# A transformer block on one core: the second feed-forward product with tokens on partitions, and the last norm along the row

## The chip, the cores and the metric

The kernel runs on one NeuronCore of a Trainium2 chip. The metric is the device time of one execution in microseconds, as the median of three runs. PE is the tensor engine (PEld its weight loads), DVE the vector engine, ACT the scalar engine, POOL GpSimd, and SP the engine whose queue issues the loads.

## The reference

One block on 256 tokens of 1024 features, all in float32. What matters here is its end:

```python
    h = rmsnorm(x, g_ffn[l]) * (1 + scale2) + shift2
    x = x + gate2 * (jnp.square(jax.nn.relu(h @ w_ff1[l])) @ w_ff2[l])   # 1024 -> 4096 -> 1024
return rmsnorm(x, g_final)                                              # per token, times g_final per feature
```

`gate2` is a vector over the 1024 features (a product of a condition vector with a weight matrix). Ahead of it stand a first norm, attention in one block of 256 keys, a gated unit and an output projection.

## The kernel before

Activations lie turned: features on partitions, tokens in the row. `x_sb` is 128 x (8, 256): eight feature tiles of 256 tokens. Every weight chunk of 128 x 2048 float32 (1 MB) is loaded by SP into `raw` (five buffers), rounded by ACT to `whi`, and the rest is taken by DVE as `wlo`; activations are split in the same way, and `mm3` adds three products in the rounded type: high by high, high by low, low by high.

The feed-forward runs in 16 units of 256 hidden features. `ff1` makes one unit's hidden sums (48 products of 258 columns), `relu2` turns them on DVE and ACT into `fh`, `relu2_low` into `fl`, each 128 x (2, 256), and `ff2` adds that unit's part of the second product to four banks `acc` that stay open over all units. The order on PE is written out in the loop: `ff1` of unit n + 3 follows `ff2` of unit n. Of one unit, `ff2` before makes 48 products: for each of eight feature tiles and two halves of the hidden features, 128 x 128 of the weight is the stationary operand, and 256 tokens of `fh` or `fl` are streamed.

```python
            for i in range(2):
                w = slice(1024 * i + P * ft, 1024 * i + P * ft + P)
                mm3(o, wh[:, w], wl[:, w], fh[:, i], fl[:, i], first and i == 0 and ft % 2 == 0,
                    last and i == 1, skip_group_check=ft % 2 == 1)
```

The last two units run by pairs of feature tiles, so that one bank after the other is complete. After each bank DVE adds gate times sum to `x_sb`, ACT squares it, and the final gain is applied per partition (`yg`). Then sixteen transposes on PE put tokens on partitions, products of one column by `ones` add the squares over the features, `rstd` takes 1/rms on ACT and POOL, and ACT and DVE each scale two quarters of the output (`ys`), which SP stores in four DMAs.

Engines issue their instructions in order. In the first part and in the tail their order is that of the code; between, a scheduler orders ACT, DVE and PE. Tiles get their waits from the framework, which follows who wrote and read a buffer.

Of the kernel before, what the change touches and what calls it, by code (L numbers as in the profile page):

```python
# [9 lines left out]
F32 = mybir.dt.float32  # L10
# [6 lines left out]
P = 128  # L17
S = 256
# [16 lines left out]
class InOrder:  # L35
    """An engine whose instructions are issued in the order in which they are traced."""
# [11 lines left out]
def block_kernel(ctx, tc, xT, cols, wsguT, bsgu, w_a1, w_1, w_a, w_m, w_f, out):  # L48
# [7 lines left out]
    los = ctx.enter_context(tc.tile_pool(name="los", bufs=3))  # L56
    ps = ctx.enter_context(tc.tile_pool(name="ps", bufs=8, space=bass.MemoryType.PSUM))
# [27 lines left out]
    # keeps the tensor engine's clock up while the first loads are under way  # L85
# [14 lines left out]
    # causal mask of one diagonal block, twice side by side: 0 where key <= query  # L100
# [87 lines left out]
    # the middle's weight chunks, and the adaLN chunks that are used beside them  # L188
# [178 lines left out]
    def wide(n, ah, al, nk, base=0):  # L367
        """Two tiles of features from one chunk, tokens in the row."""
# [46 lines left out]
    def attn_turn(pr):  # L415
        # transposed probabilities: [keys 0:128 x queries 0:256 | keys 128:256 x queries 128:256]
# [48 lines left out]
    A0, S0, TD, OD = 1, 5, 2, 3  # when attention and the gating unit start; lags of transposes and products  # L465
# [146 lines left out]
    def ff2(n, fts, wp, a, first, last):  # L612
        wh, wl = wp
        fh, fl = a
        if not acc:
            acc.extend(bank() for _ in range(4))
        for ft in fts:
            o = acc[ft // 2][:, S * (ft % 2):S * (ft % 2) + S]
            for i in range(2):
                w = slice(1024 * i + P * ft, 1024 * i + P * ft + P)  # L620
                mm3(o, wh[:, w], wl[:, w], fh[:, i], fl[:, i], first and i == 0 and ft % 2 == 0,
                    last and i == 1, skip_group_check=ft % 2 == 1)
# [12 lines left out]
    rs2 = rstd(ss2, D)  # L635
    slot += 1
# [9 lines left out]
    for n in range(NU - 2):  # L646
# [17 lines left out]
    sq3 = act.tile([P, 2, S], F32, name="sq3", tag="u1")  # L664
    yg = act.tile([P, KT, S], F32, name="yg", tag="b1")
    ss3 = bank()
    sqs = []
    for j in range(4):
        fts = (2 * j, 2 * j + 1)
        for n in (NU - 2, NU - 1):  # L670
            ff2(n, fts, parts[slot + n - NU + 2], a[n], False, n == NU - 1)
        sq = sq3 if j == 0 else wk.tile([P, 2, S], F32, name="sqt", tag="t512a")
        for i, ft in enumerate(fts):
            DVE.scalar_tensor_tensor(out=x_sb[:, ft], in0=acc[j][:, S * i:S * i + S], scalar=gcol[:, 1, ft:ft + 1],
                                     in1=x_sb[:, ft], op0=ALU.mult, op1=ALU.add)
            if j == 3:
                ACT.activation(out=sq[:, i], in_=x_sb[:, ft], func=AF.Square)
        if j < 3:
            ACT.activation(out=sq, in_=x_sb[:, 2 * j:2 * j + 2], func=AF.Square)
            if j:  # L680
                DVE.tensor_tensor(out=sq3, in0=sq3, in1=sq, op=ALU.add)
            if j == 2:
                nc.gpsimd.tensor_tensor(out=sq3[:, 0], in0=sq3[:, 0], in1=sq3[:, 1], op=ALU.add)
        for ft in fts:
            g = cols_sb[:, G_FIN + ft:G_FIN + ft + 1]
            if j < 3:
                ACT.activation(out=yg[:, ft], in_=x_sb[:, ft], func=AF.Copy, scale=g)
            else:
                DVE.tensor_scalar(out=yg[:, ft], in0=x_sb[:, ft], scalar1=g, scalar2=None, op0=ALU.mult)
# [7 lines left out]
    for ft in range(4):  # L697
        turn(ft)
# [60 lines left out]
```

## Time and profile before

| | |
|---|---|
| median of three runs | 376.34 us (376.22 to 376.67) |
| span of the profiled execution, first to last instruction | 374.8 us |
| what lies around that span, against the median | 1.5 us |
| busy PE, DVE, ACT, POOL in the span | 358.4, 266.4, 206.0, 15.4 us |
| mean granted clock of TensorE | 0.990 |
| last product of the feed-forward issued at | 365.48 us |

The profile gives the span of one execution and no other time of it; the median lies 1.5 us above, and a change in the span is read as a change in the median. A product's bar in the trace is longer than its place in the stream (they overlap in a pipeline), so that the cost of one is the distance from its start to the next one's start.

### The profile page before, as it was taken

What the parts mean: (1) busy time and instruction counts of PE and PEld (TensorE: products, weight loads), DVE (VectorE), ACT (ScalarE), POOL (GpSimd) and SP (SyncE); (2) the same over time, 40 slices, a digit from 0 to 9 for tenths busy, and PEclk for the clock granted to TensorE, in tenths of its full rate; (3) what the DMA queues carried; (4) which work ended last, traced back from release to release, by engine and by line L of the source; (5) the groups of instructions that cost most, each with busy time, mean ns of one, the idle gap of its engine ahead of it and who ended that gap; (6) DMA issues with size and microseconds to landing.
All of it is one profiled execution on the core that took longest, in us unless ns stands there. A gap on an engine that the chain in (4) does not pass through costs nothing.

```text
span 374.8 us, 6928 instructions
## 1 busy us (share of the span) xinstructions
PE 358.4 (96%) x2884; PEld 346.5 (92%) x2884; DVE 266.4 (71%) x420; ACT 206.0 (55%) x283; POOL 15.4 (4%) x21
## 2 busy tenths in 40 slices
PE   4779999999999999999999999999999999999993
PEld 3469989999899999999999999999999999999993
DVE  2899997687989986899856755766656545546442
ACT  4424346999894374356566544655445645446242
POOL 1460000010000000000000000000000000000001
PEclk9999999999999999999999999999999999999997
DMA  7999999987789995467755494764856554500003
GB/s 246 410 348 346 346 348 398 320 321 259 269 309 357 353 396 226 152 232 282 251 210 189 150 334 147 299 231 150 299 202 257 217 201 147 215 1 2 2 0 112
DMA packets 16126, 89.34 MB, mean 238 GB/s; under 512 B 1888, under 2 KB 2400, under 8 KB 7136
## 3 DMA queue, kind: packets, MB, share of 16 engines
q1 hardware_dynamic: 16096, 88.92, 64.9%
q8 instruction: 22, 0.36, 0.4%
q14 instruction: 8, 0.07, 0.0%
HBM read 87.86 MB, written 1.05 MB: 237 GB/s over the span
## 4 chain that ended last, share of the span: by engine, by line
PE 92%; issue 3%; DVE 3%; POOL 1%; POOLq 0%; DVEq 0%; ACT 0%
PE bank L44 92%; DVE junk L44 1%; DVE wlo L44 1%; POOL rs L120 0%; DVE hl L44 0%; DVE ys L44 0%; POOLq L755 0%; DVEq L755 0%; DVE acol L44 0%; DVE xn L44 0%; POOL maskf L103 0%; DVE maskf L44 0%; DVE idle L44 0%; ACT ms L44 0%; DVE ones L44 0%
## 5 line engine op out<-in xcount | busy, mean ns | idle before, releaser
L44 ACT CAST whi<-raw 128x2048 fp32r<-128x2048 f32 (+2 forms) x74 | 112.6, 1537 | 79.3 <-PE bank L44 77.7
L44 DVE TENSOR_TENSOR wlo<-raw,whi 128x2048 fp32r<-128x2048 f32 (+2 forms) x74 | 135.8, 1842 | 9.1 <-ACT whi L44 7.9
L44 PE MATMUL bank<-zh,whi 128*128 128x258 f32 x256 | 72.5, 283 | 0.0
L44 PE MATMUL bank<-zh,wlo 128*128 128x258 f32 x256 | 72.3, 282 | 0.0
L44 PE MATMUL bank<-zl,whi 128*128 128x258 f32 x256 | 72.2, 282 | 0.0
L44 PE MATMUL bank<-fl,whi 128*128 128x256 f32 x256 | 72.0, 281 | 0.0
L44 PE MATMUL bank<-fh,wlo 128*128 128x256 f32 x256 | 71.9, 281 | 0.0
L44 PE MATMUL bank<-fh,whi 128*128 128x256 f32 x256 | 71.9, 281 | 0.0
L44 PE MATMUL bank<-hl,whi 128*128 128x256 f32 x224 | 63.5, 283 | 2.4 <-DVE hl L44 2.4
L44 PE MATMUL bank<-hh,whi 128*128 128x256 f32 x224 | 64.5, 288 | 1.2 <-ACT hh L44 1.2
L44 PE MATMUL bank<-hh,wlo 128*128 128x256 f32 x224 | 63.3, 282 | 0.0
L44 DVE SCALAR_TENSOR_TENSOR junk<-raw,csb 128x1024 bf16<-128x1024 f32 x48 | 58.4, 1239 | 0.0
L44 PEld LDWEIGHTS bank<-fh,whi 128*128 128x128 f32 x256 | 49.1, 192 | 0.0
L44 PEld LDWEIGHTS bank<-zl,whi 128*128 128x128 f32 x256 | 48.4, 189 | 0.0
L44 PEld LDWEIGHTS bank<-zh,whi 128*128 128x128 f32 x256 | 48.3, 189 | 0.0
L44 PEld LDWEIGHTS bank<-zh,wlo 128*128 128x128 f32 x256 | 48.3, 189 | 0.0
L44 PEld LDWEIGHTS bank<-fh,wlo 128*128 128x128 f32 x256 | 48.1, 188 | 0.0
L44 PEld LDWEIGHTS bank<-fl,whi 128*128 128x128 f32 x256 | 48.0, 188 | 0.0
L44 PEld LDWEIGHTS bank<-hh,whi 128*128 128x128 f32 x224 | 42.9, 192 | 3.2 <-ACT hh L44 2.0
L44 PEld LDWEIGHTS bank<-hl,whi 128*128 128x128 f32 x224 | 42.7, 191 | 3.3 <-DVE hl L44 2.9
L44 PEld LDWEIGHTS bank<-hh,wlo 128*128 128x128 f32 x224 | 42.8, 191 | 0.0
L44 DVE TENSOR_TENSOR fl<-r,fh 128x512 fp32r<-128x512 f32 x16 | 11.1, 694 | 30.2 <-PE bank L44 28.9
(132 smaller groups left out, 488.7 us busy)
## 6 DMA issues: line engine op xcount, KB each, us to landing
raw<-in_w_f SPq DMA_DIRECT2D x32, 1024.0 KB, 4.8
raw<-in_w_a SPq DMA_DIRECT2D x22, 1024.0 KB, 5.8
raw<-in_w_m SPq DMA_DIRECT2D x16, 1024.0 KB, 6.5
raw<-in_w SPq DMA_DIRECT2D x12, 512.0 KB, 6.6
raw<-in_w_a SPq DMA_DIRECT2D x4, 512.0 KB, 6.8
raw<-in_w SPq DMA_DIRECT2D x8, 256.0 KB, 7.2
x_sb<-in_xT SPq DMA_DIRECT2D x2, 512.0 KB, 5.2
raw<-in_w_m SPq DMA_DIRECT2D x4, 256.0 KB, 6.8
```

Source lines behind the costliest of these rows:

```text
L44: return lambda *a, **k: pin(op(*a, **k))
```

## The change

- `ff2` swaps its operands. Now 128 tokens of `fh` or `fl` are stationary, and 512 columns of the weight are streamed; the sum has tokens on partitions. Its blocks are (token tile, first column, width): (0, 0, 512), (0, 512, 512), (1, 0, 512), (1, 512, 256), (1, 768, 256), the last two in one bank. A unit has 18 products of 512 columns and 12 of 256 in place of 48 of 256.
- The residual must lie with tokens on partitions too: sixteen transposes of `x_sb` and four ACT copies to `x1`, after ff1 of the first unit.
- Gate and final gain are needed along the row, on every partition: `gcol` goes to DRAM in pieces of one element (`g2d`), and comes back spread over the partitions (`g2row`); `gfrow` is a spread load of the gain.
- The tail runs by blocks: DVE multiplies by the gate, adds the residual and multiplies by the gain; ACT squares and sums along the row; per token tile DVE and POOL take 1/rms, ACT and DVE scale half a row each, and ACT's and SP's queue store one half each.

```diff
-        for ft in fts:
-            o = acc[ft // 2][:, S * (ft % 2):S * (ft % 2) + S]
+        if not acc:
+            acc.extend([bank(), bank()] for _ in range(2))
+        for t, c, w in blocks:
+            o = acc[t][c // 512][:, c % 512:c % 512 + w]
+            tk = slice(P * t, P * t + P)
             for i in range(2):
-                w = slice(1024 * i + P * ft, 1024 * i + P * ft + P)
-                mm3(o, wh[:, w], wl[:, w], fh[:, i], fl[:, i], first and i == 0 and ft % 2 == 0,
-                    last and i == 1, skip_group_check=ft % 2 == 1)
+                cs_ = slice(D * i + c, D * i + c + w)
+                mm = ((fh, wh), (fl, wh), (fh, wl))
+                for p, (x, y) in enumerate(mm):
+                    PE.matmul(out=o, lhsT=x[:, i, tk], rhs=y[:, cs_], start=first and i == 0 and p == 0 and c % 512 == 0,
+                              stop=last and i == 1 and p == 2, skip_group_check=c % 512 > 0)
+
+    BLOCKS = [[(0, 0, 512), (0, 512, 512)], [(1, 0, 512), (1, 512, 256), (1, 768, 256)]]
...
     rs2 = rstd(ss2, D)
+    x1 = act.tile([P, 2, D], F32, name="x1", tag="b1")
+    for t in range(2):
+        for h in range(2):
+            o = bank()
+            for ft in range(4):
+                PE.transpose(out=o[:, P * ft:P * ft + P], in_=x_sb[:, 4 * h + ft, P * t:P * t + P], identity=ident)
+            ACT.copy(out=x1[:, t, 512 * h:512 * h + 512], in_=o)
...
-        ff2(n, range(KT), parts[slot], a.pop(n), n == 0, False)
+        ff2(n, BLOCKS[0] + BLOCKS[1], parts[slot], a.pop(n), n == 0, False)
...
+        if n == 7:
+            g2d = dr.tile([KT, P], F32, name="g2d")
+            nc.sync.dma_start(out=g2d.rearrange("k p -> p k"), in_=gcol[:, 1])
+            g2row = act.tile([P, D], F32, name="g2row", tag="q1")
+            nc.sync.dma_start(out=g2row, in_=g2d.rearrange("(o k) p -> o (k p)", o=1).broadcast_to([P, D]))
+            gfrow = act.tile([P, D], F32, name="gfrow", tag="q2")
+            nc.sync.dma_start(out=gfrow, in_=gfin.broadcast_to([P, D]))
...
+    y = act.tile([P, 2, D], F32, name="y", tag="b2")
+    yg = act.tile([P, 2, D], F32, name="yg", tag="b3")
+    for t in range(2):
+        blocks = BLOCKS[t]
+        ssq = const.tile([P, len(blocks)], F32, name="ssq", tag=f"ssq{t}")
+        for k, (t, c, w) in enumerate(blocks):
+            for n in (NU - 2, NU - 1):
+                ff2(n, [(t, c, w)], parts[slot + n - NU + 2], a[n], False, n == NU - 1)
+            cw = slice(c, c + w)
+            DVE.tensor_tensor(out=y[:, t, cw], in0=acc[t][c // 512][:, c % 512:c % 512 + w], in1=g2row[:, cw],
+                              op=ALU.mult)
+            DVE.tensor_tensor(out=y[:, t, cw], in0=y[:, t, cw], in1=x1[:, t, cw], op=ALU.add)
+            junk = wk.tile([P, 512], F32, name="junk2", tag="t512a")
+            ACT.activation(out=junk[:, 0:w], in_=y[:, t, cw], func=AF.Square, accum_out=ssq[:, k:k + 1])
+            DVE.tensor_tensor(out=yg[:, t, cw], in0=y[:, t, cw], in1=gfrow[:, cw], op=ALU.mult)
+        ms = wk.tile([P, 1], F32, name="ms", tag="ms")
+        mj = wk.tile([P, len(blocks)], F32, name="mj", tag="mj")
+        DVE.tensor_scalar(out=mj, in0=ssq, scalar1=1.0 / D, scalar2=EPS, op0=ALU.mult, op1=ALU.add, accum_out=ms)
+        rs = wk.tile([P, 1], F32, name="rs", tag="rs")
+        nc.gpsimd.tensor_tensor(out=rs, in0=ms, in1=nhalf[:, 0:1], op=ALU.pow)
+        ACT.activation(out=yg[:, t, 0:512], in_=yg[:, t, 0:512], func=AF.Copy, scale=rs)
+        nc.scalar.dma_start(out=out[t][:, 0:512], in_=yg[:, t, 0:512])
+        DVE.tensor_scalar(out=yg[:, t, 512:D], in0=yg[:, t, 512:D], scalar1=rs, scalar2=None, op0=ALU.mult)
+        nc.sync.dma_start(out=out[t][:, 512:D], in_=yg[:, t, 512:D])
```

The first place is PE at the end of the first unit's `ff1`. Here and below a name is a tile with its number, and a wait in brackets names the engine (or DMA queue) whose semaphore is waited for. Before:

```order
L44 MATMUL bank_2158<-zh_1865,wlo_2007 128x258
L44 MATMUL bank_2150<-ones_97,sq2_1869 128x1 [waits DVE_49,PE_49]
L44 MATMUL bank_2150<-ones_97,sq2_1869 128x1
L44 MATMUL bank_2221<-zh_1865,whi_1938 128x258 [waits PE_49]
L44 MATMUL bank_2221<-zl_1866,whi_1938 128x258
L44 MATMUL bank_2221<-zh_1865,wlo_2080 128x258
```

After, in the same place:

```order
L44 MATMUL bank_2160<-zh_1867,wlo_2009 128x258
L44 MATMUL bank_2152<-ones_99,sq2_1871 128x1 [waits DVE_49,PE_49]
L44 MATMUL bank_2152<-ones_99,sq2_1871 128x1
L44 MATMUL bank_2216<-ident_103,x_sb_80 128x128 [waits DMAHW1_49,PE_49]
L44 MATMUL bank_2216<-ident_103,x_sb_80 128x128 x3
L44 MATMUL bank_2222<-ident_103,x_sb_80 128x128 [waits DMAHW2_49]
L44 MATMUL bank_2222<-ident_103,x_sb_80 128x128 x3
L44 MATMUL bank_2228<-ident_103,x_sb_80 128x128 x4
L44 MATMUL bank_2234<-ident_103,x_sb_80 128x128 x4
L44 MATMUL bank_2248<-zh_1867,whi_1940 128x258
L44 MATMUL bank_2248<-zl_1868,whi_1940 128x258
L44 MATMUL bank_2248<-zh_1867,wlo_2082 128x258
```

Sixteen transposes stand between the sums of squares and the second unit's `ff1`, and wait for loads of the head and for PE itself alone.

The second place is PE in the tail, where the last two blocks meet: (1, 512, 256) ends and (1, 768, 256) begins, both in `bank_2395`.

```order
L44 MATMUL bank_2395<-whi_3708,fh_3843 128x256
L44 MATMUL bank_2395<-whi_3708,fl_3852 128x256
L44 MATMUL bank_2395<-wlo_3806,fh_3843 128x256
L44 MATMUL bank_2395<-whi_3652,fh_3745 128x256 [waits DVE_49]
L44 MATMUL bank_2395<-whi_3652,fl_3808 128x256
L44 MATMUL bank_2395<-wlo_3754,fh_3745 128x256
```

The first product of the last block waits for DVE. In the tail before, no product of the four banks after the first waits for another engine.

The third place is DVE in the tail. Before, with `bank_2366` to `bank_2368` the last three banks of the sum:

```order
L44 SCALAR_TENSOR_TENSOR x_sb_78<-bank_2366,gcol_156,x_sb_78 128x256 [waits PE_49]
L44 SCALAR_TENSOR_TENSOR x_sb_78<-bank_2366,gcol_156,x_sb_78 128x256
L44 TENSOR_TENSOR sq3_4073<-sq3_4073,sqt_4129 128x512 [waits Activation_49]
L44 SCALAR_TENSOR_TENSOR x_sb_78<-bank_2367,gcol_156,x_sb_78 128x256 [waits PE_49]
L44 SCALAR_TENSOR_TENSOR x_sb_78<-bank_2367,gcol_156,x_sb_78 128x256
L44 TENSOR_TENSOR sq3_4073<-sq3_4073,sqt_4160 128x512 [waits Activation_49]
L44 SCALAR_TENSOR_TENSOR x_sb_78<-bank_2368,gcol_156,x_sb_78 128x256 [waits PE_49]
L44 SCALAR_TENSOR_TENSOR x_sb_78<-bank_2368,gcol_156,x_sb_78 128x256
L44 TENSOR_SCALAR yg_4074<-x_sb_78,cols_sb_76 128x256 [waits DVE_49] x2
L44 TENSOR_SCALAR ys_4229<-bank_4201,rs_4227 128x512 [waits PE_49,Pool_49]
L44 TENSOR_SCALAR ys_4229<-bank_4202,rs_4227 128x512 [waits PE_49]
```

After, from the second block of token tile 0 (`bank_2393`) to the last block's first instruction:

```order
L44 TENSOR_TENSOR y_3854<-bank_2393,g2row_3276 128x512 [waits PE_49]
L44 TENSOR_TENSOR y_3854<-y_3854,x1_2215 128x512 [waits DVE_49]
L44 TENSOR_TENSOR yg_3855<-y_3854,gfrow_3278 128x512 [waits DVE_49]
L44 TENSOR_SCALAR mj_3892,ms_3891<-ssq_3856 128x2 [waits Activation_49]
L44 TENSOR_SCALAR yg_3855<-yg_3855,rs_3894 128x512 [waits Pool_49]
L44 TENSOR_TENSOR y_3854<-bank_2394,g2row_3276 128x512 [waits PE_49]
L44 TENSOR_TENSOR y_3854<-y_3854,x1_2215 128x512 [waits DVE_49]
L44 TENSOR_TENSOR yg_3855<-y_3854,gfrow_3278 128x512 [waits DVE_49]
L44 TENSOR_TENSOR y_3854<-bank_2395,g2row_3276 128x256 [waits PE_49]
L44 TENSOR_TENSOR y_3854<-y_3854,x1_2215 128x256 [waits DVE_49]
L44 TENSOR_TENSOR yg_3855<-y_3854,gfrow_3278 128x256 [waits DVE_49]
L44 TENSOR_TENSOR y_3854<-bank_2395,g2row_3276 128x256 [waits PE_49]
```

Between the two tiles' work there now stand two instructions of tile 0, of which one waits for ACT and one for POOL, and tile 1's first instructions are queued behind them. The read of `bank_2395` at 256 columns comes fourth after these.

## Rows read from the trace of the kernel before

**Rows 1.** The page, its first line.
```profile
span 374.8 us, 6928 instructions
```

**Rows 2.** Chain that ended last: start us, us, what.
```profile
26.07 341.85 PE bank L44 x2807
```

**Rows 3.** Window: us, busy PE, PEld, DVE, ACT, POOL (x), granted clock, DMA, GB/s.
```profile
230.00:340.00 110.00, 110.00 (x928) 110.00 (x927) 65.57 (x84) 57.18 (x57) 0.00 (x0) 1.00 0.53 192
```

**Rows 4.** Timeline of PE, one second-product unit: start us, us, engine line op.
```profile
200.35 0.28 PE L44 MATMUL bank<-fh,whi 128*128 128x256 f32 x1
...
206.00 0.28 PE L44 MATMUL bank<-zh,whi 128*128 128x258 f32 x1
```

**Rows 5.** Timeline of PE, twelve 512-column products of phase 1.
```profile
52.91 0.39 PE L44 MATMUL bank<-whi,hh 128*128 128x512 f32 x1
...
55.48 0.40 PE L44 MATMUL bank<-wlo,hh 128*128 128x512 f32 x1
```

**Rows 6.** Timeline of all engines, from the last product to the output.
```profile
365.48 0.28 PE L44 MATMUL bank<-fh,wlo 128*128 128x256 f32 x1
...
365.61 1.03 PE L44 MATMUL bank<-ident,yg 128*128 128x128 f32 x8
...
365.81 0.88 DVE L44 SCALAR_TENSOR_TENSOR x_sb<-bank,gcol,x_sb 128x256 f32<-128x256 f32 x2 [0.56 <-PE bank L44]
...
366.48 0.50 PE L44 MATMUL bank<-ones,sq 128*128 128x1 f32 x4
...
368.35 0.71 POOL L120 TENSOR_TENSOR rs<-ms,nhalf 128x2 f32<-128x2 f32 x1 [2.29 <-ACT ms L44]
369.09 1.41 DVE L44 TENSOR_SCALAR ys<-bank,rs 128x512 f32<-128x512 f32 x2 [1.88 <-POOL rs L120]
369.80 1.81 SPq L712 DMA_DIRECT2D out_dram<-ys  x4
```

**Rows 7.** Timeline of ACT: start us, us, engine line op [idle before <-releaser].
```profile
191.92 0.37 ACT L44 COPY rb<-bank 128x256 f32<-128x256 f32 x1 [1.81 <-PE bank L44]
```

**Rows 8.** Groups of instructions: xcount | busy us, mean ns of one | idle.
```profile
L44 ACT COPY v_sb<-bank 128x512 f32<-128x512 f32 x2 | 1.1, 621 | 0.0
L44 DVE SCALAR_TENSOR_TENSOR yg<-gb_sb,bank 128x512 f32<-128x512 f32 x4 | 2.8, 688 | 4.5 <-PE bank L44 4.5
L44 DVE TENSOR_TENSOR r<-bank,rb 128x256 f32<-128x256 f32 x32 | 13.2, 415 | 1.8 <-ACT rb L44 1.8
L44 ACT ACTIVATE vj<-vs_sb 128x512 f32<-128x512 f32 x2 | 1.2, 632 | 0.0
L44 ACT ACTIVATION_READ_ACCUMULATOR vj<-vs_sb 128x1 f32 x2 | 0.4, 201 | 0.0
L44 DVE TENSOR_SCALAR yg<-x_sb,cols_sb 128x256 f32<-128x256 f32 x2 | 0.6, 346 | 0.0
L44 DVE TENSOR_SCALAR vms<-vss 128x2 f32<-128x2 f32 x1 | 0.2, 170 | 2.4 <-ACT vj L44 2.4
L44 ACT ACTIVATE sqt<-x_sb 128x256 f32<-128x256 f32 x2 | 0.7, 416 | 1.1 <-DVE x_sb L44 1.1
```

**Rows 9.** Timeline of DVE, SP and ACT, in the feed-forward.
```profile
284.32 0.22 DVE L44 TENSOR_SCALAR gcol<-acc,cols_sb 128x1 f32<-128x1 f32 x1
288.96 0.33 SPq L66 DMA_DIRECT2D raw<-in_w_f  x1
308.75 1.92 ACT L44 CAST whi<-raw 128x2048 fp32r<-128x2048 f32 x1 [0.93 <-PE bank L44]
```

**Rows 10.** DMA issues: xcount, KB each, median us to landing.
```profile
raw<-in_w_f SPq DMA_DIRECT2D x32, 1024.0 KB, 4.8
cols_sb<-in_cols SPq DMA_DIRECT2D x1, 42.0 KB, 1.7
```

**Rows 11.** Busy time per engine and granted clock, columns as in rows 3.
```profile
23.00:26.07 3.07, 0.70 (x4) 0.19 (x2) 2.96 (x8) 2.18 (x3) 1.39 (x2) 1.00 0.89 315
26.25:29.65 3.40, 3.40 (x17) 3.40 (x18) 3.39 (x7) 0.13 (x1) 0.00 (x0) 0.50 0.82 283
```

More of the change, by code (lines that the diff above doesn't have):

```diff
@@ L47, in block_kernel @@
 @with_exitstack
-def block_kernel(ctx, tc, xT, cols, wsguT, bsgu, w_a1, w_1, w_a, w_m, w_f, out):
+def block_kernel(ctx, tc, xT, cols, wsguT, bsgu, w_a1, w_1, w_a, w_m, w_f, gfin, out):
     nc = tc.nc
@@ L56, in block_kernel @@
     los = ctx.enter_context(tc.tile_pool(name="los", bufs=3))
+    dr = ctx.enter_context(tc.tile_pool(name="dr", bufs=1, space=bass.MemoryType.DRAM))
     ps = ctx.enter_context(tc.tile_pool(name="ps", bufs=8, space=bass.MemoryType.PSUM))
@@ L610, in block_kernel, with ff2 @@
     acc = []
-    def ff2(n, fts, wp, a, first, last):
+    def ff2(n, blocks, wp, a, first, last):
         wh, wl = wp
@@ L615, in ff2 @@
         if not acc:
-            acc.extend(bank() for _ in range(4))
-        for ft in fts:
-            o = acc[ft // 2][:, S * (ft % 2):S * (ft % 2) + S]
+            acc.extend([bank(), bank()] for _ in range(2))
+        for t, c, w in blocks:
+            o = acc[t][c // 512][:, c % 512:c % 512 + w]
+            tk = slice(P * t, P * t + P)
             for i in range(2):
-                w = slice(1024 * i + P * ft, 1024 * i + P * ft + P)
-                mm3(o, wh[:, w], wl[:, w], fh[:, i], fl[:, i], first and i == 0 and ft % 2 == 0,
-                    last and i == 1, skip_group_check=ft % 2 == 1)
+                cs_ = slice(D * i + c, D * i + c + w)
[4 more added lines that the diff above has]
+    BLOCKS = [[(0, 0, 512), (0, 512, 512)], [(1, 0, 512), (1, 512, 256), (1, 768, 256)]]
     f = {}
@@ L662, in block_kernel @@
     PE.pinned = DVE.pinned = ACT.pinned = True
[L664 to L689, printed above, removed]
@@ L690, in block_kernel @@
-    ob = [[bank() for _ in range(2)] for _ in range(2)]
-    def turn(ft):
-        for t in range(2):
-            PE.transpose(out=ob[t][ft // 4][:, P * (ft % 4):P * (ft % 4) + P], in_=yg[:, ft, P * t:P * t + P],
-                         identity=ident)
-    for ft in range(4):
-        turn(ft)
-    for q, first, last in ((sq3[:, 0], True, False), (sq[:, 0], False, False), (sq[:, 1], False, True)):
-        sums(ss3, q, first, last)
-    for ft in range(4, KT):
-        turn(ft)
-    rs3 = rstd(ss3, D)
@@ L704, in block_kernel @@
-    ys = act.tile([P, 2, D], F32, name="ys", tag="b2")
-    for h in range(2):
-        for t in range(2):
-            y = ys[:, t, 512 * h:512 * h + 512]
-            if t == 0:
-                ACT.activation(out=y, in_=ob[t][h], func=AF.Copy, scale=rs3[:, t:t + 1])
-            else:
-                DVE.tensor_scalar(out=y, in0=ob[t][h], scalar1=rs3[:, t:t + 1], scalar2=None, op0=ALU.mult)
-            nc.sync.dma_start(out=out[t][:, 512 * h:512 * h + 512], in_=y)
+    y = act.tile([P, 2, D], F32, name="y", tag="b2")
@@ L746 @@
         "w_f": np.stack([wf1, wf2], axis=1).reshape(2 * NU, P, 2048),
+        "gfin": a["g_final"].reshape(1, D),
     }
```

## The prediction

> **What bounds the kernel now.** I read the page's first line for the span [rows 1], then the chain of waits, which follows the last instruction back to what released it: from 26.07 us on, 341.85 us of it are products on PE with nothing between them [rows 2]. The table by windows says the same of the feed-forward: from 230 to 340 us PE is busy for 110.00 us of 110.00 at a granted clock of 1.00, the 2.4 GHz level, with DVE at 66 us and ACT at 57 [rows 3]. So until the last product only PE's own time counts, every product added there costs its place in the stream, and what DVE, ACT and the loads get is free while PE never waits for them. After the last product at 365.48 a chain over ACT, POOL, DVE and SP sets the end [rows 6]. I therefore cost the change in three parts: PE's stream, the tail, and whatever could make PE wait.
>
> **The second product.** Before, the 48 products of a unit take from 200.35 to 206.00, that is 5.65 / 48 = 0.1177 us each [rows 4]. For the new form phase 1 has the very shape, 128 activation columns stationary and 512 weight columns streamed: eleven steps from 52.91 to 55.48, 0.2336 us each [rows 5]. Two old products (0.2354) against one new (0.2336) save 1.8 ns. A unit trades 36 old ones for 18 and keeps 12 of 256 columns; 18 x 16 = 288 trades x 1.8 ns = **-0.5 us**. The rows are rounded to 0.01 us, which leaves 0.2 to 0.8. Half as many weight loads bring nothing else, since PE's stream was closed already.
>
> **The residual's transposes.** Sixteen go into PE's closed stream after the first unit's `ff1`. Eight such transposes in the old tail take from 365.61 to 366.48, 0.109 us each [rows 6]: 16 x 0.109 = **+1.7 us**. They wait for nothing that is late, so I take no more; less than 1.6 is excluded, since nothing idles on PE there. The sixteen transposes that leave stood in the tail and are counted there. The four ACT copies to `x1` are at most 0.62 us each, 2.5 in all [rows 8], and are hidden: ACT sat idle for 1.81 us before copying `rb` [rows 7], and that copy comes 1.7 us later now. Were this cover gone, `rb2` would be late, next `relu2` of the first unit, and only then `ff2`.
>
> **The tail.** I lay both tails on one clock that starts with the first product of the last two units. Before: 96 products, the last at 95 x 0.1177 = 11.18, so zero is 365.48 - 11.18 = 354.30, and SP's last output issue ends at 369.80 + 1.81 = 371.61 [rows 6], which is 17.31.
>
> After, token tile 0: its 24 products of 512 columns end with one issued at 23 x 0.2336 = 5.37. DVE read a finished sum 0.33 us after its last product's start (365.48 to 365.81 [rows 6]); a product of 512 columns lasts 0.11 longer (0.39 against 0.28 [rows 4, 5]): 5.81. Multiply and add at 0.69 each: 7.19. ACT 0.1 later, square and reading of its sum 0.63 + 0.20 less a 0.1 overlap: 8.02. DVE's mean, 0.17 by the nearest row and a sum to read: 8.30. POOL after 0.1, 0.71 long: 9.11 [rows 6, 8]. Then DVE's scaling of 512 columns in SBUF, which the trace lacks: 256 columns in SBUF take 0.35 [rows 8], 512 from PSUM half of 1.41 [rows 6]; between them I take 0.55: 9.69.
>
> Now the queue matters. DVE takes its instructions in order, and tile 1's first block, whose last product was issued at 35 x 0.2336 = 8.18 and which could be read at 8.6, stands behind that scaling. Its three instructions take 3 x 0.69: 11.76. Only then comes the read of block (1, 512, 256), 0.41 long: 12.17. The last block lies in the same bank, and its first product waits for DVE (the order's second place), so PE goes on at 12.2. With no wait it would have gone on at 8.18 + 0.23 + 12 x 0.1177 = 9.82. **PE stands still for 2.4 us.** What is late next is the last block itself.
>
> This is where the Trainium skill speaks against the change: "PSUM — Partial Sum Buffer", in its section on bank collisions, asks that accesses be guarded by whole banks, not by addresses, and so that a bank be read only while products go to another. By that rule halves of one bank cannot overlap and the wait is needed; without it the sum would come out as in the fourth rival. The trace of before has no such wait in its tail, whose reads and writes go to different banks.
>
> From there: last product 12.2 + 11 x 0.1177 = 13.5; DVE at 13.84, two instructions of 0.41 with a handover: 14.7; ACT 0.1 later, 0.42 and the sum's reading: 15.35; DVE's mean: 15.6; POOL: 16.4; ACT's scaling at 0.69: 17.15; its DMA issue of 0.41: 17.6 at most. Against 17.31: **+0.3 us**. The transposes, sums and two-step output that go (about 2 us) are paid back by the standstill. Bounds: the scaling between 0.35 and 0.7 moves it by 0.2 either way. Two last stores on two queues, where four shared one, land in between 0 and 0.5 us less; no row tells, and I take 0.
>
> **The side loads** are put at nothing. The gate's last column is ready at 284.54 [rows 9], and `g2d` is issued then. Its 1024 runs of four bytes land in between 1.7 us, as 128 short runs do, and eight times that, 13.6 [rows 10]. SP holds `g2row` back for it, and behind it the load that before was issued at 288.96; ACT casts that load at 308.75, after a wait for PE [rows 9]. With 4.8 us to land [rows 10] there are 15.0 us of cover, and even the upper end holds the queue only until 298.1, a delay of 9.2. If the cover were gone, ACT's casts would be late, and `relu2` behind them. `gfrow` is issued among the loads before the feed-forward and waits for a product long done when needed.
>
> **Sum.** -0.5 + 1.7 + 0.3 = +1.5 us: a span of 374.8 + 1.5 = 376.3, and against the median 376.34 + 1.5 = **377.8 us**, 0.4% slower. The measurement can tell 0.2% (0.75 us) from no change.
>
> **The rivals.** *The clock falls in the tail.* At 23 to 26 us PE stood idle for 2.37 us of 3.07, and from 26.25 to 29.65 the granted clock was 0.50, the 1.2 GHz level, with 17 products in 3.40 us, 0.20 each [rows 11]. A standstill of 2.4 us is as much. If the clock falls right after it, up to 12 products of 256 columns cost 0.08 more: up to +1.0, 378.8 us. It can also fall too late to touch them. Chance 0.25.
>
> *The standstill is shorter.* If the scaling needs 0.35 us, POOL's handovers are quicker and the two stores land 0.5 earlier, 0.7 to 1.2 us go: 376.6 to 377.1, within 0.2%. Chance 0.15.
>
> *The side loads hold up PE.* If `g2d` took over 19 us (303.96 less 284.54) in place of at most 13.6, ACT's casts would wait, say 379. Nothing in the rows points there. Chance 0.04.
>
> *PE does not wait for DVE between the last two blocks* (the faster side). The change would then be worth what it removes: +1.5 - 2.4 = -0.9, 375.4 us. It decides once the standstill is under 0.15 us for faster by over 0.2%, at 0.9 for no loss. The order of DVE and the wait on PE speak against it; for it, only that the two halves are different addresses. Chance 0.08.
>
> *The wide products are faster than in phase 1.* 256 columns at 2.4 GHz are 0.1067 us; the row has 0.0110 more. If that were paid per instruction, each trade would save it: 288 x 0.0110 = 3.2 us in place of 0.5, 375.1 us. The 0.2336 of phase 1 speaks against it. Chance 0.03. The Trainium skill, "TensorE: Matmul & The Clock Gate", section "Wait — 56ns, not 53.3ns?", has columns / 2.4 GHz plus a fixed 2.5 ns, so 0.2158 for 512; by it against the old 0.1177 a trade would save 0.0196, 5.6 us, and the estimate from that page would be 372.7. The trace disagrees: both rows lie above it, and in proportion to the columns.
>
> **How the numbers follow.** The forecast case has 0.45; its own range is 377.1 to 378.4 (products 0.3, scaling 0.2, stores and handovers the rest). Range 376.5 to 379.0: it takes in the clock's case and the shorter standstill, and leaves out the two faster ones and part of the loads, about 0.15. Slower by over 0.2% than before: 0.45 + 0.25 + 0.04 = 0.74; within: 0.15; faster: 0.08 + 0.03 = 0.11.
>
> **What the profile after would show.** 288 products of 512 columns 0.233 us apart in `ff2`; sixteen transposes in 1.7 us after the first unit; the last product at the end of the span's stream preceded by an idle PE of about 2.4 us that DVE ends; a granted clock of 1.00 or 0.50 behind it; the output's first DMA issued on ACT. I am wrong if PE's idle time before the last block is under 1 us, if the wide products are 0.22 apart or less, or if ACT casts wait for loads.

## The result, and the profile after

The changed kernel takes 379.35 us (median of four runs, 378.91 to 380.65), the kernel before 376.5 beside it (376.22 to 376.99): a ratio of 1.0079, 95% interval 1.0059 to 1.0098, some 2.9 us slower. The forecast was 377.8 with a range of 376.5 to 379.0. The direction was right; about half of the loss was not foreseen.

The page of the changed kernel: its first line [rows 1], the busy times, ScalarE's casts, and the one group of products in the feed-forward that waits for VectorE (xcount | busy us, mean ns | idle before them and its releaser).

```profile
span 377.6 us, 6344 instructions
...
PE 358.6 (95%) x2584; PEld 334.3 (89%) x2584; DVE 269.4 (71%) x427; ACT 206.1 (55%) x285; POOL 15.1 (4%) x21
...
L44 ACT CAST whi<-raw 128x2048 fp32r<-128x2048 f32 (+2 forms) x74 | 112.5, 1536 | 79.3 <-PE bank L44 78.1
...
L44 PE MATMUL bank<-whi,fh 128*128 128x512 f32 (+1 forms) x160 | 55.9, 349 | 1.9 <-DVE y L44 1.9
```

The span grew by 2.75 us (374.84 to 377.59), and PE's closed stream now has one hole, of 1.9 us. To see where the rest went I cut both spans at the same instructions: the last wide product of phase 1, the first product that reads `oh`, `mh`, `zh` (the activations that the two output projections and the feed-forward multiply), the sums, the second unit's `ff1`, the first `ff2` product, the last `ff1` product (between these two lie 13 units, called the `ff2` loop below; the 14th unit's `ff2` follows), the first product of the last two units, the last product of all. Windows between these marks, columns as in [rows 3]; first of the kernel before:

```profile
66.73:136.59 69.86, 69.86 (x609) 66.37 (x608) 59.71 (x109) 53.93 (x99) 1.79 (x2) 1.00 0.87 321
136.71:159.33 22.62, 22.62 (x195) 22.62 (x194) 17.32 (x17) 10.18 (x9) 0.00 (x0) 1.00 0.61 224
159.33:182.21 22.88, 22.88 (x195) 22.68 (x194) 22.09 (x37) 12.46 (x16) 0.00 (x0) 1.00 0.75 268
...
187.96:188.32 0.36, 0.36 (x6) 0.36 (x5) 0.16 (x1) 0.28 (x1) 0.00 (x0) 1.00 1.23 523
...
200.35:348.52 148.17, 148.17 (x1249) 148.17 (x1248) 88.70 (x116) 78.04 (x78) 0.00 (x0) 1.00 0.52 188
354.29:365.48 11.19, 11.19 (x97) 11.19 (x96) 4.71 (x9) 4.29 (x9) 0.16 (x1) 1.00 0.00 0
365.48:374.84 9.36, 3.36 (x31) 3.12 (x29) 2.81 (x6) 2.27 (x5) 1.28 (x2) 0.79 0.30 112
```

and the same stretches of the changed kernel, with the one that now holds the transposes:

```profile
66.60:137.62 71.02, 71.02 (x610) 67.53 (x609) 59.66 (x109) 54.05 (x99) 1.80 (x2) 1.00 0.87 322
137.74:160.78 23.04, 23.04 (x195) 23.04 (x194) 17.33 (x17) 10.18 (x9) 0.00 (x0) 1.00 0.59 202
160.78:183.98 23.20, 23.20 (x194) 23.08 (x193) 22.11 (x37) 12.44 (x16) 0.00 (x0) 1.00 0.78 292
189.78:191.84 2.06, 2.06 (x22) 2.06 (x21) 1.86 (x1) 1.99 (x3) 0.00 (x0) 1.00 0.79 330
...
203.89:351.65 147.76, 147.76 (x1016) 137.41 (x1014) 88.70 (x116) 77.97 (x78) 0.00 (x0) 1.00 0.58 192
357.37:370.65 13.28, 11.40 (x62) 9.55 (x60) 8.66 (x16) 3.40 (x9) 0.55 (x1) 1.00 0.10 39
370.65:377.59 6.94, 0.35 (x3) 0.07 (x1) 1.92 (x6) 1.23 (x3) 0.55 (x1) 0.51 0.20 76
```

The reader is to see three things. **The first three pairs** hold code that the change does not touch, with equal counts (to the one product that a window's edge takes in), PE busy throughout and a granted clock of 1.00 in both; yet they are 1.16, 0.42 and 0.32 us longer. In the second pair 192 products of 256 columns follow each other: 22.62 / 192 = 117.8 ns before, 23.04 / 192 = 120.0 after. **The transposes** cost 2.06 - 0.36 = 1.70 us (the old stretch, of the two sums alone, is 187.96 to 188.32). **`ff2`'s loop** is 0.41 shorter, and the two tails are 11.19 + 9.36 = 20.55 against 13.28 + 6.94 = 20.22. With the small pieces between them: -0.13 (first 67 us) + 1.96 (unchanged products up to the sums) + 1.70 - 0.44 (loop, the `ff1` ahead of it and the 14th unit's `ff2` behind it) - 0.33 = +2.76.

The timeline around the standstill and at the end, of the changed kernel (start us, us, engine line op [idle before <-releaser]):

```profile
365.71 0.55 POOL L706 TENSOR_TENSOR rs<-ms,nhalf 128x1 f32<-128x1 f32 x1 [172.89 <-DVE mj L44]
...
366.30 0.48 DVE L44 TENSOR_SCALAR yg<-yg,rs 128x512 f32<-128x512 f32 x1 [0.76 <-POOL rs L706]
...
366.70 0.68 DVE L44 TENSOR_TENSOR y<-bank,g2row 128x512 f32<-128x512 f32 x1
...
367.07 0.28 PE L44 MATMUL bank<-wlo,fh 128*128 128x256 f32 x1
367.42 0.69 DVE L44 TENSOR_TENSOR y<-y,x 128x512 f32<-128x512 f32 x1
...
368.14 0.69 DVE L44 TENSOR_TENSOR yg<-y,gfrow 128x512 f32<-128x512 f32 x1
...
368.75 0.42 DVE L44 TENSOR_TENSOR y<-bank,g2row 128x256 f32<-128x256 f32 x1
...
369.22 0.39 PE L44 MATMUL bank<-whi,fh 128*128 128x256 f32 x1 [1.88 <-DVE y L44]
...
370.65 0.35 PE L44 MATMUL bank<-wlo,fh 128*128 128x256 f32 x1
...
374.23 0.34 ACTq L708 DMA_DIRECT2D out_dram<-yg  x1
```

PE issues the last product of block (1, 512, 256) at 367.07 and the next one, into the same bank, at 369.22, just after VectorE has read the first half (368.75 + 0.42). VectorE came to that read late, as forecast: scaling of tile 0, then three instructions of the block before. Without the wait the next product would have stood at 367.19, so the standstill is 2.03 us.

### The profile page after: what moved, and what is told of

Same layout as the page of the kernel before. It is cut to its first block, busy times and chain, and to the rows that moved or that the text cites. A ratio compares the mean times of both kernels' runs of the same rounds, so it can differ in the third digit from the quotient of the medians.

```text
span 377.6 us, 6344 instructions
## 1 busy us (share of the span) xinstructions
PE 358.6 (95%) x2584; PEld 334.3 (89%) x2584; DVE 269.4 (71%) x427; ACT 206.1 (55%) x285; POOL 15.1 (4%) x21
## 4 chain that ended last, share of the span: by engine, by line
PE 90%; DVE 4%; issue 3%; POOL 1%; ACT 0%; POOLq 0%; DVEq 0%; ACTq 0%
PE bank L44 90%; DVE y L44 1%; DVE junk L44 1%; DVE wlo L44 1%; POOL rs L121 0%; DVE hl L44 0%; DVE yg L44 0%; ACT junk L44 0%; ACT yg L44 0%; DVE acol L44 0%; POOLq L754 0%; POOL rs L706 0%; DVE xn L44 0%; POOL maskf L104 0%; DVE mj L44 0%
## 5 line engine op out<-in xcount | busy, mean ns | idle before, releaser
L44 ACT CAST whi<-raw 128x2048 fp32r<-128x2048 f32 (+2 forms) x74 | 112.5, 1536 | 79.3 <-PE bank L44 78.1
L44 PE MATMUL bank<-hl,whi 128*128 128x256 f32 x224 | 64.3, 287 | 2.5 <-DVE hl L44 2.5
L44 PE MATMUL bank<-whi,fh 128*128 128x512 f32 (+1 forms) x160 | 55.9, 349 | 1.9 <-DVE y L44 1.9
L44 PE MATMUL bank<-wlo,fh 128*128 128x512 f32 (+1 forms) x160 | 56.0, 350 | 0.0
L44 PE MATMUL bank<-whi,fl 128*128 128x512 f32 (+1 forms) x160 | 55.8, 349 | 0.0
L44 PEld LDWEIGHTS bank<-hl,whi 128*128 128x128 f32 x224 | 43.7, 195 | 3.3 <-DVE hl L44 3.0
L44 PEld LDWEIGHTS bank<-hh,wlo 128*128 128x128 f32 x224 | 43.6, 195 | 0.0
L44 PEld LDWEIGHTS bank<-whi,fh 128*128 128x128 f32 x160 | 30.1, 188 | 6.3 <-DVE y L44 2.1
L44 PEld LDWEIGHTS bank<-whi,fl 128*128 128x128 f32 x160 | 30.1, 188 | 4.3
L44 PEld LDWEIGHTS bank<-wlo,fh 128*128 128x128 f32 x160 | 30.0, 188 | 4.3
```

What stands on the lines that cost most here:

```text
L44: return lambda *a, **k: pin(op(*a, **k))
```

## The experiments

Runs of one kernel spread over some 5 us here (before: 373.11 to 378.36 in one set of 29). The profiles show where: the last wide product of phase 1 starts between 63.60 and 66.91 us in them, while the stretches after it repeat to 0.1 us where the code is the same. So I give the timed ratio with its interval, and beside it the stretches, in us:

| stretch | before | after | e1 | e2 | e3 | e7 | e8 | e9 | e11 |
|---|---|---|---|---|---|---|---|---|---|
| rest of phases 1 and 2 | 69.86 | 71.02 | 71.02 | 69.86 | 71.02 | 69.87 | 69.86 | 69.87 | 69.86 |
| `oh`, `yh` products | 22.61 | 23.04 | 23.04 | 22.61 | 23.04 | 22.61 | 22.61 | 22.61 | 22.61 |
| `mh` products | 22.88 | 23.21 | 23.21 | 22.88 | 23.21 | 22.88 | 22.88 | 22.19 | 22.88 |
| sums, transposes | 0.36 | 2.06 | 0.36 | 2.06 | 2.06 | 2.06 | 2.06 | 2.06 | 0.36 |
| `ff2` loop | 148.17 | 147.76 | 149.47 | 146.78 | 147.39 | 146.17 | 146.78 | 145.66 | 149.64 |
| last two units, to the last product | 11.19 | 13.28 | 11.40 | 13.15 | 10.97 | 10.76 | 12.33 | 10.65 | 11.40 |
| from there to the end | 9.36 | 6.94 | 9.20 | 6.92 | 7.66 | 7.80 | 6.98 | 7.85 | 9.35 |

**My theory for the unforeseen 1.96 us: addresses.** The change adds two tiles `ssq` and a tile `mj`, and these push every tile allocated after them along. Bytes in each partition, from the two compiled programs:

```
            oh      hh      zh      fh      whi     wlo
before   46784   54976   71360  117824   168320  201088
after    46848   55040   71424  117888   168448  201216
```

The differences of addresses that are named below are worked out from these. The rivals are the chip or the run, and contention with the new loads (though the difference starts long before the first new instruction).

**e1, the kernel before at the addresses of after.** No product is changed.

```diff
+    for n in range(2):
+        nc.gpsimd.memset(const.tile([P, 2], F32, name="pad", tag=f"pad{n}"), 0.0)
+        nc.gpsimd.memset(wk.tile([P, 2], F32, name="pad", tag="padw"), 0.0)
```

> The kernel before, with no product changed: two small constant tiles and one small working tile are added, cleared by four tiny GpSimd instructions ahead of the tail, so that every later tile lies at the SBUF address that it has in the changed kernel. Theory (the products' own pace follows the addresses of their operands): the products of 256 columns in the stages up to the feed-forward, 117.7 ns apart before and 120.0 after the change, are 120.0 ns apart here too; the first sums of the feed-forward stage start 1.8 us later than before, and the whole takes 378 to 381 us, as the 768 products of 256 columns of the old second product may slow down too. Rival (the 1.8 us came from the chip or the run, or from the changed instructions): 376.5 us, 117.7 ns, no shift at the sums.

380.27 us, ratio 1.0127 (1.0087 to 1.0167). Two windows of its profile:

```profile
135.94:158.98 23.04, 23.04 (x194) 23.04 (x193) 17.32 (x17) 10.18 (x9) 0.00 (x0) 1.00 0.58 212
...
200.40:349.87 149.47, 149.47 (x1250) 149.47 (x1249) 88.66 (x115) 77.96 (x78) 0.00 (x0) 1.00 0.50 186
```

The first three stretches have the lengths of the changed kernel to 0.01 us, and the loop is 1.30 us longer than before. (The sums start no later on the clock, since this execution's first wide product came 1.7 us earlier.) The four clearing instructions run at 1.0 us, at the very start and not ahead of the tail, 0.1 us each. Unused tiles alone slow the old kernel down.

**e2, the changed kernel at the addresses of before.**

```diff
-        ssq = const.tile([P, len(blocks)], F32, name="ssq", tag=f"ssq{t}")
+        ssq = wk.tile([P, len(blocks)], F32, name="ssq", tag="sm", bufs=2)
-        mj = wk.tile([P, len(blocks)], F32, name="mj", tag="mj")
+        mj = wk.tile([P, len(blocks)], F32, name="mj", tag="rc", bufs=2)
```

> The changed kernel, with its three new small tiles put into working buffers that exist already, so that every later tile lies where it lay before the change. Theory (addresses): products of 256 columns before the feed-forward are 117.7 ns apart again, and 1.8 us go: 377.3 to 377.7 us, close to the 377.8 of the prediction. Rival (not the addresses): 379.35 us as the changed kernel, 120.0 ns.

375.06 us, ratio 0.9989 (0.9959 to 1.0018).

```profile
133.59:156.20 22.61, 22.61 (x195) 22.61 (x193) 17.32 (x17) 10.17 (x9) 0.00 (x0) 1.00 0.61 220
...
198.89:345.67 146.78, 146.78 (x1015) 137.06 (x1014) 88.70 (x115) 78.05 (x78) 0.00 (x0) 1.00 0.57 193
```

The old paces are back, and more than I had expected: the loop, too, is 0.98 us shorter than in the changed kernel, 0.73 of it since the wide products are 229.3 ns apart here and 232.6 there. With e1, which ran on the same chip beside it and shows the other pace, this settles the theory: the same edit without the shift costs nothing that can be measured.

**e5, the changed kernel once more**, as a control.

> The changed kernel itself once more, beside the other runs, since single executions spread over some 4 us here while their products keep their pace to the nanosecond from the 40th microsecond on. Theory: ratio to the kernel before 1.008 as first measured, and from the last 512-column product of the first stage on the same times as in the first trace within 0.1 us, so that all spread lies in the first 67 us. Rival: the spread lies in the feed-forward or the tail.

378.71 us, ratio 1.0071 (1.0047 to 1.0096). Its stretches are those of the first trace (71.02, 23.04, 23.21, 147.76; the tail 13.37 and 7.00), and its last wide product of phase 1 starts 1.66 us earlier. Its span is 1.50 us shorter: what sets these two executions apart lies in the first 67 us, all but 0.15 us in the tail.

**e6, the products by themselves**, at 256 pairs of offsets with 256 columns and 128 pairs with 512.

```diff
+    for m in range(0, 512, 32):
+        for w in range(0, 512, 32):
+            products(8, 256, m, w)
...
+            PE.matmul(out=banks[k[0] % 2][:, 0:cols], lhsT=sta[:, w // 4:w // 4 + P], rhs=mov[:, m // 4:m // 4 + cols],
+                      start=True, stop=True)
```

> PE's products by themselves: the block is left out (the output is not the reference's), and after two loads and two copies nothing runs but float32r products from one tile of 4096 streamed columns and one of 4096 stationary columns, with no wait between them and no other engine busy. Eight products of 256 columns follow each other at each pair of offsets, 0 to 480 bytes by 32 for either operand, then multiples of 512 bytes up to 8192 for one of them, then five products of 512 columns at offsets by 32 and 64. Theory (the pace follows the addresses): the mean distance of two products of 256 columns depends on the pair, between about 115 and 123 ns, with multiples of 64 bytes that are no multiple of 128 unlike multiples of 128, and shows pairs faster than the 117.7 of the kernel before. Rival (other engines or transfers set it): one pace at all pairs, within 0.5 ns.

Windows of the pairs with a streamed offset of 0 (128 products), of the multiples of 512 bytes (256 products), and of all 512-column pairs (640):

```profile
23.27:38.45 15.18, 15.18 (x130) 15.18 (x129) 0.00 (x0) 0.00 (x0) 0.00 (x0) 1.00 0.00 1
265.93:296.64 30.71, 30.71 (x258) 30.71 (x257) 0.00 (x0) 0.00 (x0) 0.00 (x0) 1.00 0.00 1
296.64:444.73 148.09, 148.09 (x641) 120.06 (x640) 0.00 (x0) 0.00 (x0) 0.00 (x0) 1.00 0.00 1
```

15.18 / 128 = 118.6 ns on average; 30.71 / 256 = 120.0 where the two operands differ by a multiple of 512 bytes; with no other engine and no transfer at work. The pace follows mostly the difference of the two addresses, stationary less streamed, and repeats mostly every 256 bytes. Median (and range) over the pairs with the same difference, in ns from one product's start to the next, worked out from the starts; at difference 0 the median for 256 columns is that of the pairs up to 480 bytes (118.2 to 119.2), and the 120.0 is that of the multiples of 512 bytes:

```
difference mod 256      0      32      64      96     128     160     192     224
256 columns         118.2   118.5   117.8   117.8   118.8   120.0   117.8   117.8
  lowest            118.2   117.5   115.8   117.7   118.3   118.0   117.7   117.3
  highest           120.0   118.5   117.8   120.5   119.0   120.0   117.8   117.8
512 columns         226.7   232.8   232.7   234.5   230.3   231.5   233.3   233.3
  lowest            226.7   231.0   232.3   234.0   230.3   231.3   228.7   233.3
  highest           232.0   234.0   234.0   235.7   235.3   234.7   233.3   233.7
```

The old kernel's `oh` products have a difference of 192 (117.8), the changed one's of 0 (120.0); phase 1's wide products had 64 in the kernel before, 232.7 here and 233.6 in [rows 5]. It is not the whole rule: e2's wide products stand at 192 and run at 229.3, near the lowest of that column, not its median, and e1's `ff2` at 128 runs at 120.0 on average, over its column's highest. The changed kernel's own wide products stand at 128 and run at 232.6 where the median is 230.3, so that by the medians the changed kernel's would be the faster ones and e2's the slower, and in the kernels it is the other way. That addresses set the pace is shown; which difference is best for a kernel this table does not tell.

**e11, an address moved on purpose, in the kernel before**: the activations of `ff2` go from a difference of 64 to one of 0.

```diff
-        fh = wk.tile([P, 6 * P], F32R, name="fh", tag="pr", bufs=3)[:, 0:512].rearrange("p (i t) -> p i t", i=2)
+        fh = wk.tile([P, 6 * P], F32R, name="fh", tag="pr", bufs=3)[:, 16:528].rearrange("p (i t) -> p i t", i=2)
...
-        fl = wk.tile([P, 6 * P], F32R, name="fl", tag="pt")[:, 0:512].rearrange("p (i t) -> p i t", i=2)
+        fl = wk.tile([P, 6 * P], F32R, name="fl", tag="pt")[:, 16:528].rearrange("p (i t) -> p i t", i=2)
```

> The same edit as in e9, in the kernel before: its activations of the old second product move 64 bytes, so that they and the weights differ by 0 in place of 64 bytes modulo 256. Theory (e6: 256 columns at a difference of 0 are 118.2 to 120.0 ns apart, at 64 bytes 117.8): the 768 products of the old second product go from 117.8 to 118.5 or up to 120 ns apart, 0.5 to 1.7 us more from the first of them on, so that the edit that shortens the one kernel lengthens the other; ratio 1.001 to 1.005. Rival: no change of pace, ratio 1.000.

378.52 us, ratio 1.0040 (1.0013 to 1.0068).

```profile
200.50:350.14 149.64, 149.64 (x1250) 149.64 (x1248) 88.68 (x115) 77.96 (x78) 0.00 (x0) 1.00 0.51 186
356.01:367.41 11.40, 11.40 (x97) 11.40 (x96) 4.70 (x9) 4.30 (x9) 0.21 (x1) 1.00 0.00 0
```

The products of `ff2` are 119.9 ns apart in place of 117.8, the loop 1.47 us longer, the 14th unit's `ff2` 0.10 and the last two units 0.21, in all 1.78, just over the 1.7 that I gave as the upper end; all stretches before it are unchanged.

**e4, without the transposes.** The residual is left out of the output.

```diff
-            o = bank()
-            for ft in range(4):
-                PE.transpose(out=o[:, P * ft:P * ft + P], in_=x_sb[:, 4 * h + ft, P * t:P * t + P], identity=ident)
-            ACT.copy(out=x1[:, t, 512 * h:512 * h + 512], in_=o)
+            nc.gpsimd.memset(x1[:, t, 512 * h:512 * h + 512], 0.0)
```

> The changed kernel without the sixteen transposes of the residual and their four copies: the residual tiles are cleared by GpSimd, so the residual is left out of the output. Theory (each instruction in PE's stream costs its place): the start of the first second-product comes 1.7 us earlier and the whole takes 1.7 us less, 377.6 us. Rival (the transposes displace waits that would come anyway): less than 0.8 us goes, 378.6 us or more.

378.01 us, ratio 1.0066 (1.0037 to 1.0094).

```profile
190.05:190.42 0.37, 0.37 (x7) 0.37 (x5) 0.17 (x1) 0.29 (x1) 0.00 (x0) 1.00 0.99 421
202.47:350.22 147.75, 147.75 (x1015) 137.41 (x1014) 88.68 (x115) 77.98 (x78) 0.00 (x0) 1.00 0.57 192
355.94:369.27 13.33, 11.41 (x62) 9.55 (x60) 8.66 (x16) 3.41 (x9) 0.56 (x1) 1.00 0.10 39
```

The timed ratio does not show the gain: 1.70 us would put it near 1.0026 beside e5's 1.0071, and that lies outside its interval. The stretches of the profiled execution are clear: 2.06 becomes 0.36, and the loop (147.75) and the last two units (13.33) keep their length, so nothing downstream gives the 1.70 us back. What the timed executions lack would have to lie in the first 67 us, which vary; that it does is not shown.

**e3, no shared bank.** Tile 1's second half is one block of 512 columns in every unit.

```diff
-    BLOCKS = [[(0, 0, 512), (0, 512, 512)], [(1, 0, 512), (1, 512, 256), (1, 768, 256)]]
+    BLOCKS = [[(0, 0, 512), (0, 512, 512)], [(1, 0, 512), (1, 512, 512)]]
```

> The changed kernel, with token tile 1's second half as one block of 512 columns in place of two of 256 that share a bank, in every unit. Theory (the standstill is the shared bank, behind the order of VectorE's instructions): PE's idle time of 1.9 us ahead of the last block goes altogether, the last product comes about 2 us earlier, VectorE's queue then holds the end back by some of it, and the span is 0.8 to 1.5 us shorter, with 0.3 us more from 96 pairs of products of 256 columns that become 96 of 512: 377.6 to 378.4 us. Rival (VectorE's queue sets the end with or without the shared bank): the idle time goes but the time stays at 379.1 or above.

376.22 us, ratio 1.0027 (1.0002 to 1.0052), 0.44% under e5's; PE has no wait in the tail.

```profile
356.80:367.77 10.97, 10.97 (x49) 8.82 (x47) 6.98 (x13) 2.38 (x6) 0.56 (x1) 1.00 0.06 24
367.77:375.43 7.66, 0.40 (x2) 0.00 (x0) 3.16 (x7) 1.97 (x5) 0.55 (x1) 0.73 0.27 102
```

The last two units take 10.97 (13.28), the stretch behind them 7.66 (6.94), since VectorE's last pieces are 512 wide; the loop is 0.37 shorter. In all 1.97 us less, above the 0.8 to 1.5 and 0.3 that I gave.

**e8, the shared bank kept, VectorE's order changed**, at the addresses of before.

```diff
-        DVE.tensor_scalar(out=yg[:, t, 512:D], in0=yg[:, t, 512:D], scalar1=rs, scalar2=None, op0=ALU.mult)
+        if t == 0:
+            ACT.activation(out=yg[:, t, 512:D], in_=yg[:, t, 512:D], func=AF.Copy, scale=rs)
+        else:
+            DVE.tensor_scalar(out=yg[:, t, 512:D], in0=yg[:, t, 512:D], scalar1=rs, scalar2=None, op0=ALU.mult)
```

> The changed kernel at the addresses of before, with the shared bank kept, and tile 0's scaling of the second half moved from VectorE to ScalarE, so that VectorE's queue does not wait for GpSimd's power there. Theory (VectorE's order makes the standstill long, the shared bank makes it a standstill): PE's idle time ahead of the last block falls from 1.9 to 1.1 to 1.3 us and the span by 0.5 to 0.8 us against e2 from the first product of the last two units on. Rival (the bank alone, by the read of its first half, sets it): idle time of 1.8 us or more. Second rival: ScalarE's longer queue delays the end by as much, and only the idle time falls.

375.37 us, ratio 0.9970 (0.9942 to 0.9997). The lists of waits (PE, waited for: us in total, times, longest) have one row each from 300 us on, first e2's, then this run's:

```profile
PE bank L44 <- DVE y L44: 1.9, 1, 1.9
```

```profile
PE bank L44 <- DVE y L44: 1.2, 1, 1.2
```

The idle time is 1.2 us against e2's 1.9, the last two units 12.33 against 13.15, the end 6.98 against 6.92. So the shared bank makes the standstill (in e3 it is gone), and VectorE's queue stretches it by 0.8.

**e7, the two repairs together** (e2's and e3's edits).

> The changed kernel at the addresses of before (small tiles in buffers that exist) and with token tile 1's second half as one block of 512 columns. Theory (the two gains add): from e2's 375.06 about 2 us go (1.6 in the tail as in e3, 0.4 to 0.7 in the loop, where 96 pairs of 256 columns become products of 512 at 229 to 231 ns): 372.8 to 373.5 us, ratio to the kernel before 0.992 to 0.995. Rival (addresses and standstill overlap): 374.5 us or more.

374.01 us, ratio 0.9928 (0.9902 to 0.9954): faster than both kernels. The ratio is inside the range that I gave, the median 0.5 us over it and under the rival's.

```profile
202.12:348.29 146.17, 146.17 (x937) 133.21 (x936) 88.72 (x115) 77.96 (x78) 0.00 (x0) 1.00 0.58 194
353.92:364.68 10.76, 10.76 (x49) 8.82 (x47) 6.88 (x13) 2.27 (x6) 0.56 (x1) 1.00 0.05 20
```

Loop 146.17, last two units 10.76, end 7.80; against before -2.00 in the loop, -1.99 in the tail and +1.70 for the transposes. The gains add.

**e9, e7 with e11's edit**, which here takes the wide products to a difference of 0.

> e7 with one edit: the two activation tiles of the second product begin 16 columns (64 bytes) later inside their buffers, so that they and the weights differ by 0 in place of 192 bytes modulo 256. Theory (e6: 512 columns at a difference of 0 are mostly 226.7 ns apart, the lowest of the table): the 384 wide products go from 229.2 to about 227 ns apart, 0.8 us less, ratio to the kernel before 0.988 to 0.992, no other stretch changed. Rival (the pace in the kernel is set by something else than that difference): 229.2 ns and e7's time.

373.22 us, ratio 0.9933 (0.9906 to 0.9960). The wide products are 227.6 ns apart (229.2 in e7) and the loop is 145.66, 0.51 shorter, with the 14th unit's `ff2` and the last two units 0.66: the edit that lengthened the old kernel shortens this one, by a little less than the 0.8 that I gave.

```profile
201.45:347.11 145.66, 145.66 (x938) 133.18 (x936) 88.68 (x116) 77.98 (x78) 0.00 (x0) 1.00 0.58 195
```

The timed ratio misses my 0.988 to 0.992 and does not tell e9 from e7. Against the forecast a stretch ahead of the edit changed too, the `mh` products (last section); whether what made that stretch faster also touched the wide products is not shown.

**e10, e9 with e8's edit.**

> e9 with tile 0's scaling of the second half on ScalarE. Theory: without the shared bank PE waits for nothing there, and VectorE, which reaches the last block within 0.1 us of its last product in e7, gains little: 0 to 0.3 us less than e9 after the last product. Rival (VectorE's wait for GpSimd is on the path): 0.5 us or more.

373.40 us, ratio 0.9930 (0.9908 to 0.9952). After the last product 7.77 us against 7.85: with no shared bank VectorE's order costs 0.1.

## Why the prediction was right and wrong, point by point

**The step that failed** ends the prediction's first paragraph: "I therefore cost the change in three parts: PE's stream, the tail, and whatever could make PE wait", after "only PE's own time counts, every product added there costs its place in the stream". That PE's own time counts held: from 67 us to the tail it is busy without a break in the kernels before and after. But the three parts take for granted that the products which stay keep their pace; a change of it was put at nothing without a word. They did not keep it: 1.96 us came in code that the diff does not touch, because three small tiles moved the operands. e1 shows it without any of the change, e2 takes it away, e6 shows the pace to depend on the addresses with nothing else running, and e11 slows the old products by an address alone. None of my three signs of being wrong could show it, as all three looked at the change's own instructions: PE idled for 1.88 us, the wide products were 0.233 us apart, and no cast of the feed-forward waited for a load. The difference between after and e2 is 3.2 us in the stretches from 67 us on, more than the whole loss.

**The wide products** (-0.5 forecast): -0.46 in the loop and the 14th unit's `ff2` behind it. The agreement is half luck. In the loop 234 trades saved 0.72 us, 3.1 ns each where I had 1.8, and the products that stay, `ff1` above all, took 0.31 of it back. The price from phase 1 was 233.6 ns, but phase 1 itself ran at 229 in the changed kernel and `ff2` at 232.6; at the old addresses the same trade is worth -1.50 (e2: -1.39 and -0.11). The rival "wide products are faster than in phase 1", put at 0.03, held in part there. Its far end did not: by the estimate from the Trainium skill, "TensorE: Matmul & The Clock Gate", section "Wait — 56ns, not 53.3ns?", 512 columns take 215.8 ns; the lowest pair of e6 is 226.7, so the measurement decides against it at every address tried.

**The transposes** (+1.7): 1.70, and e4's profile shows that nothing behind them gives it back. Their copies were hidden, as said.

**The tail** (+0.3) measured -0.33; the mechanism was right and the terms were too large. The standstill is 2.03 against 2.4: GpSimd took 0.55 for one column and not the 0.71 of the row with two, VectorE's scaling 0.48 and not 0.55, and VectorE's instructions overlap a little. On the clock that starts with the last two units SP's or ACT's last issue ends at 374.57 - 357.37 = 17.20 (forecast 17.6, before 17.31), and the two stores land 0.21 us sooner behind it, which I had put at 0 with bounds of 0 and 0.5. The rule that I set beside this step, the Trainium skill's "PSUM — Partial Sum Buffer" in its section on bank collisions, asks for accesses to be guarded by whole banks; the program holds such a wait, and PE idled for 1.88 us in it. Whether the halves could be written and read at once was not tried. One small thing was the other way round: the output's first DMA was issued on SP, at 366.81, and ACT's at 367.05.

**The rivals.** The clock did fall behind the standstill, but too late to touch the products, as I had left open: it stands at 1.00 through the 1.88 us of idle PE up to the last product at 370.65, and at 0.51 behind it. In e5 it fell a little sooner (0.83 from 368.40 to the last product at 369.08), and the last two units took 13.37 in place of 13.28. The side loads held up nothing: ACT's wait for PE, 78.1 us on the page, is still the largest before its casts, and no cast of the feed-forward waits for a load. `g2d` took 10.0 us to land, inside my 1.7 to 13.6, and SP waited 9.0 us for it; but the load that I had put behind that wait left ahead of it, at 288.33, and only the next one behind it, at 298.36. "PE does not wait for DVE" is excluded by the 1.88 us. "The standstill is shorter" held as far as the tail goes, and could not show in the time, since the addresses cost more than it gave. No rival had the addresses.

**My sum by its own terms** is therefore -0.46 + 1.70 - 0.33 = +0.91 where I had +1.5; the 1.96 that I had not seen, less 0.13 in the first 67 us, makes 2.74 of the span's 2.75.

## What to carry to other kernels

Where PE's stream is closed, a new tile of a few bytes can cost more than the edit that needs it: compare the pace of unchanged products before and after, and put small tiles into buffers that exist (e2), or allocate them last, which no run here tried. A term priced from one row at one address may be off by 2 or 3% elsewhere, which over two thousand products is more than this whole change. And where the halves of a bank share one wait, PE has to wait, before it sums the second half, for the reader of the first and for all that stands in the reader's queue; one wide block was faster here.

## What the runs showed that I had not expected

The same pair of addresses can run at two paces. In e9 and e10 the last 152 products of the `mh` stretch are 113.3 ns apart, in the kernel before and in e7 117.8, with equal addresses for all 192. The edit of e9 comes later: up to the first `ff2` product its program is that of e7. The stretch in e9 and in e7:

```profile
159.45:181.64 22.19, 22.19 (x195) 21.99 (x193) 21.99 (x37) 12.46 (x16) 0.00 (x0) 1.00 0.81 297
```

```profile
159.43:182.30 22.87, 22.87 (x194) 22.67 (x193) 22.09 (x37) 12.45 (x16) 0.00 (x0) 1.00 0.79 292
```

Behind one product that is 222 or 223 ns from the next, the pace is 113.3 in e9 and 117.8 in e7. So something beside the addresses and the order of the program matters too; what it is stays open, and the tables above are what was seen, not a rule that gives every pace. The `oh` products, by contrast, were 117.8 ns apart in all seven profiles at the old addresses and 120.0 in all five at the new ones.

Second, the first 67 us vary from profile to profile by up to 3.3 us, more than this change. Where PE had stood idle in the stretch from 23 us, the granted clock was 0.50 for the next 3.4 us, the 1.2 GHz level, and 16 products were in work in that window; in e2 it was 1.00 in the same window, with 23 products:

```profile
23.00:26.02 3.02, 0.65 (x3) 0.19 (x1) 2.91 (x8) 2.17 (x3) 1.35 (x2) 0.99 0.83 269
26.02:29.40 3.38, 3.38 (x16) 3.38 (x17) 3.38 (x6) 0.31 (x1) 0.00 (x0) 0.50 0.92 315
```

```profile
26.00:29.40 3.40, 3.40 (x23) 2.98 (x22) 3.29 (x8) 1.27 (x2) 0.00 (x0) 1.00 1.03 376
```

The first fence is the changed kernel, the second e2. Phase 1's last wide product started at 63.60 in e2 and at 66.60 in the changed kernel. But the clock is not simply higher in e2: from 12 to 20 us it was 0.50 there, and 1.00 in the changed kernel. So it is where the slow stretch falls, and not only whether there is one, that differs; why is not shown.
